# Gate and up products of a SwiGLU feed-forward: both parts of x side by side in one 512-column product

## The chip, the cores and the metric

One core of one Trainium2 chip runs the whole program in one launch. The metric is the device time of one execution in microseconds (us). TensorE (PE) multiplies, VectorE (DVE) and ScalarE (ACT) do the elementwise work, GpSimd (POOL) does a little, and SyncE (SP) issues the transfers.

## The reference

Two layers on 256 positions of width 1024. Each layer has a mixer (a gMLP spatial gate in layer 0, an RWKV-7 time mixer in layer 1) between two half-step feed-forwards, and a gated embedding at its end. So there are four feed-forwards, each with weights of its own:

```python
D_MODEL = 1024
D_FF = 2816
def rms_norm(x, g):
    y = xf * lax.rsqrt(jnp.mean(xf * xf, axis=-1, keepdims=True) + RMS_EPS)
    return (y * g.astype(jnp.float32)).astype(x.dtype)

def swiglu(x, w13, w2):
    gate, up = jnp.split(x @ w13, 2, axis=-1)
    return (jax.nn.silu(gate) * up) @ w2
...
    h = h + 0.5 * rms_norm(swiglu(rms_norm(h, g[0]), ffn_w13[i, 0], ffn_w2[i, 0]), g[1])
```

Everything is float32.

## The kernel before

**Products in parts.** A float32 operand is held as two parts, a high part rounded to the format in which TensorE takes a float32 in one pass, and a low part, the rest. A product is the sum of three: high by high, low by high and high by low. The helper `mm3` (lines 162 to 166) issues these three, on lines 164, 165 and 166, into one PSUM region.

**Weights.** They come in units of 128 rows by 1024 columns (512 KB). `emit_dma` reads a unit into a raw buffer. `emit_split` makes the two parts: ACT rounds it into the first half of a 2048-column slot (line 140), DVE subtracts to get the low part into the second half (line 142). `pump(k, reserve)` emits up to k splits if enough slots are free and at most 12 units are ahead; `need(i)` makes sure that unit i has been split, and `release(i)` gives its slot back.

**A feed-forward (`ffn`).** The hidden width of 2816 is walked in 11 chunks of 256; each chunk has a gate half and an up half. A chunk takes four units of gate and up weights (`at13`) and two units of down weights (`at2`). x, already scaled by the norm's gain and transposed, lies in two slots: one with the high parts, one with the low parts, each 8 blocks of 128 rows (k) by 256 positions. Chunks 0 and 1 go through `A`, where x is the stationary operand, and `TR` transposes their result. Chunks 2 to 10 go through `AT`, where the weights are stationary and the 256 positions are the moving operand, so that the result comes out transposed. `AT` takes two PSUM banks; bank j holds gate and up (256 columns each) of 128 hidden rows. For each of 8 blocks k, two j and two i (gate, up) it issues the three products of `mm3`: 96 products of 256 columns in a chunk, 36 chunks in the four feed-forwards. Then for each j it empties the bank: DVE multiplies the 512 columns by the positions' norm factors (line 387), ACT takes the silu (line 390), DVE multiplies gate by up (line 391), and the result is split into parts by ACT (line 393) and DVE (line 394) into a ring of four chunks.

`Dn(c, b)` multiplies a chunk of the ring by the down weights, 12 products of 512 columns for one half b of the positions, into two of four `acc` banks that stay open over all chunks. In the loop `Dn(c - 2, ...)` stands behind `AT(c)`. Behind the loop come `Dn` of chunks 8, 9 and 10 for the first half, the norm of that half, and the rest.

**Order.** The program is written in the order of the calls; a scheduler may move an instruction past neighbours on its engine, and each engine then runs its list in order, with waits where data or a buffer requires them. PSUM banks and slots are given out first freed, first taken.

Of the kernel before, what the change touches and what calls it, by code (L numbers as in the profile page):

```python
# [10 lines left out]
F32R = mybir.dt.float32r  # L11
AF = mybir.ActivationFunctionType
ALU = mybir.AluOpType
# [3 lines left out]
T = 256  # L17
NB = 2
KT = 8
DFF = 2816  # L20
FC = 11
# [20 lines left out]
SE, SO = CE[3] ** 0.5, CO[2] ** 0.5  # L42
BE, BO = CE[2] / (2 * SE), CO[1] / (2 * SO)
KE, KO = CE[1] - BE * BE, CO[0] - BO * BO


class Trunk:
    NSLOT = 20

    def __init__(self, ctx, tc, io):  # L50
        self.tc = tc
        self.nc = tc.nc
        self.io = io
        self.uid = 0
        ep = lambda name, bufs=1, **k: ctx.enter_context(tc.tile_pool(name=name, bufs=bufs, **k))
        self.slots = ep("slots")
        self.pp = ep("pp", space=bass.MemoryType.PSUM)
        self.rawp = ep("raw", 4)
        self.gp = ep("gp", 2)
        self.cp = ep("cp")  # L60
        self.sp = ep("sp", 2)
        self.rcp = ep("rc")
        self.rdp = ep("rd", space=bass.MemoryType.DRAM)
        self.free = deque(f"S{i}" for i in range(self.NSLOT))
        self.banks = deque(f"P{i}" for i in range(8))
        self.held = {}
        self.units = []
        self.hl = {}
        self.raw = {}
        self.n_dma = 0  # L70
        self.n_split = 0
        self.last = False
        self.left = [0, 1]
        self.on_pool = set()
        self.rn = [None, None]
        self.pq = {}
# [203 lines left out]
    def xslots(self):  # L280
        t = [self.slot("xT", F32R) for _ in range(2)]
        v = [q.rearrange("p (k t) -> p k t", t=T) for q in t]
        return t, [[q[:, :, b * 128:(b + 1) * 128] for q in v] for b in range(NB)]


    def ffn_units(self, f):
        io = self.io
# [18 lines left out]
    def ffn(self, l, j, at, filler=None):  # L306
        nc = self.nc
        at13, at2 = at
        gcol = l * 8 + 4 * j
        xs, xT, rstd = [], [], [None, None]  # L310
        hT = {}
        acc = {}

        def start(b):
            if b == 0:
                q, v = self.xslots()
                xs.extend(q)
                xT.extend(v)
            self.transpose_split(self.h[b], xT[b], gcol)
            rstd[b] = self.rn[b]  # L320

        yield start
        nxt = yield
        rs = [self.slot("hT", F32R) for _ in range(2)]
        ring = [q.rearrange("p (r s k t) -> p r s k t", r=2, s=2, t=T) for q in rs]
        hv = lambda c: ring[c % 4 // 2][:, c % 2]
        xv = [q.rearrange("p (k t) -> p k t", t=T) for q in xs]
        hc_of = {}

        def A(c, b, mid=None):  # L330

            ps = self.bank("mm")
            for u in range(4):
                if u == 3 and mid:
                    mid(1)
                wh, wl = self.need(at13[c] + u)
                for q in range(2):
                    k = 2 * u + q
                    sl = slice(q * 512, (q + 1) * 512)
                    self.mm3(ps, xT[b][0][:, k, :], xT[b][1][:, k, :], wh[:, sl], wl[:, sl], k == 0, k == KT - 1)  # L340
                if b == 1:
                    self.release(at13[c] + u)
            if rstd[b] is None:
                self.pre_norm(b)
                rstd[b] = self.rn[b]
            sg = self.small(256, "k1", 6)
            hc = self.small(256, "k1", 6)
            nc.scalar.activation(sg, ps[:, :256], AF.Silu, scale=rstd[b])
            nc.vector.scalar_tensor_tensor(hc, ps[:, 256:], rstd[b], sg, op0=ALU.mult, op1=ALU.mult)
            self.unbank(ps)  # L350
            hc_of[c, b] = hc

        def TR(c, b):
            v = hv(c)[:, :, :, b * 128:(b + 1) * 128]
            self.transpose_split(hc_of.pop((c, b)), (v[:, 0], v[:, 1]), None, 2)

        def rows():

            ps = self.bank("rb")
            for b in range(NB):  # L360
                d = self.small(256, "k1", 6)
                nc.vector.tensor_scalar(d[:, :128], self.ident, rstd[b], None, op0=ALU.mult)
                nc.tensor.matmul(ps[:, b * 128:(b + 1) * 128], lhsT=self.ones, rhs=d[:, :128], start=True, stop=True)
            r = self.small(256, "yc", 4)
            nc.scalar.copy(r, ps[:, :T])
            self.unbank(ps)
            return r

        def AT(c):

            ps = [self.bank("mm") for _ in range(2)]
            for u in range(4):
                wh, wl = self.need(at13[c] + u)
                for q in range(2):
                    k = 2 * u + q
                    for j in range(2):
                        for i in range(2):
                            sl = slice(q * 512 + i * 256 + j * 128, q * 512 + i * 256 + j * 128 + 128)
                            self.mm3(ps[j][:, i * T:(i + 1) * T], wh[:, sl], wl[:, sl], xv[0][:, k, :], xv[1][:, k, :],
                                     k == 0 and i == 0, k == KT - 1 and i == 1)  # L380
                self.release(at13[c] + u)
                if u % 2:
                    self.pump(1, self.room)
            for j in range(2):
                z = self.small(512, "pn", 3)
                sg = self.small(256, "k1", 6)
                nc.vector.tensor_tensor(z.rearrange("p (i t) -> p i t", i=2), ps[j].rearrange("p (i t) -> p i t", i=2),  # L387
                                        rbc.unsqueeze(1).to_broadcast([128, 2, T]), op=ALU.mult)
                self.unbank(ps[j])
                nc.scalar.activation(sg, z[:, :T], AF.Silu)  # L390
                nc.vector.tensor_tensor(sg, sg, z[:, T:], op=ALU.mult)
                hi, lo = hv(c)[:, 0, j, :], hv(c)[:, 1, j, :]
                nc.scalar.copy(hi, sg)
                nc.vector.tensor_tensor(lo, sg, hi.bitcast(F32), op=ALU.subtract)

        def Dn(c, b):
            if b not in acc:
                acc[b] = [self.bank("acc") for _ in range(2)]
            v = hv(c)[:, :, :, b * 128:(b + 1) * 128]
            order = [(k, n) for k in range(2) for n in range(2)]  # L400
            if c == FC - 1:
                order.sort(key=lambda q: q[1])
            for k, n in order:
                wh, wl = self.need(at2[c] + k)
                sl = slice(n * 512, (n + 1) * 512)
                self.mm3(acc[b][n], v[:, 0, k, :], v[:, 1, k, :], wh[:, sl], wl[:, sl],
                         c == 0 and k == 0, c == FC - 1 and k == 1)
            if b == 1:
                for k in range(2):
                    self.release(at2[c] + k)  # L410

        P = lambda k: self.pump(k, self.room)
        A(0, 0); P(2); A(1, 0, start); P(1)
        g = self.gain_tile(self.io["norm_g"][l, 1 + 4 * j:2 + 4 * j, :])
        TR(0, 0)
        A(0, 1); P(2); TR(1, 0)
        rbc = rows()
        A(1, 1); P(2); TR(0, 1)
        for c in range(2, FC):
            AT(c); P(1)  # L420
            if c == 2:
                TR(1, 1)
            if c < FC - 1:
                Dn(c - 2, 0); P(2)
                if c < FC - 2:
                    Dn(c - 2, 1); P(1)
        self.drop(*xs)
        Dn(FC - 3, 0)
        Dn(FC - 2, 0)
        Dn(FC - 1, 0)  # L430
        self.post_norm(0, acc[0], g, True, acc[0])
        P(2)
        Dn(FC - 4, 1)
        P(2)
        Dn(FC - 3, 1)
        P(2)
        Dn(FC - 2, 1)
        P(2)
        nxt(0)
        Dn(FC - 1, 1)  # L440
        self.drop(*rs)
        if filler is not None:
            filler()
        self.post_norm(1, acc[1], g, True, acc[1])
        yield
# [1069 lines left out]
def layout(inp):  # L1515

    c = np.ascontiguousarray
    f = lambda k: np.asarray(inp[k])
    a = {}
# [3 lines left out]
    a["norm_g"] = g  # L1523
    a["gT"] = g.reshape(16, KT, 128).transpose(2, 0, 1).reshape(128, 128)
    w = f("ffn_w13").reshape(4, 4, 2, 128, 2, FC, 256)
    a["w13"] = w.transpose(0, 5, 1, 3, 2, 4, 6).reshape(4, FC, 4, 128, 1024)
    a["w2"] = f("ffn_w2").reshape(4, 2 * FC, 128, D)
    a["wp"] = f("ple_w_proj")
    a["wg"] = f("ple_w_gate")
# [12 lines left out]
    s, t = np.arange(N)[:, None], np.arange(N)[None, :]  # L1542
# [32 lines left out]
```

## Time and profile before

| | |
|---|---|
| time, 3 runs | 1225.7, 1227.05, 1227.19 us; median 1227.05 |
| profiled execution | 1224.77 us |
| its span, first to last instruction | 1223.0 us |
| PE busy | 1191.8 us (97%), 8526 products |
| weight loads busy | 1027.2 us (84%) |
| DVE busy | 786.3 us (64%) |
| ACT busy | 603.6 us (49%) |
| products of 256 columns in `AT` | 3 x 1152 |

Busy time of PE is the time in which at least one product is under way. Successive products overlap, so the time that one product costs is read from the distance of the starts, or from a stretch divided by its count, and not from the duration of a row.

### The profile page before, as it was taken

Reading aid. Unit: us, or ns where it says so; the run is one execution under the profiler, and the core shown is the slowest. Engines: PE = TensorE matmul, PEld = TensorE weight load, DVE = VectorE, ACT = ScalarE, POOL = GpSimd, SP = SyncE. Lnnn points to the kernel's source line nnn. Section 1 sums busy time; section 2 is a strip of 40 time slices with the busy share of each in tenths; the row PEclk is TensorE's granted clock in tenths of the full one; section 3 lists DMA queues with packets and bytes.
Section 4 is the critical chain, followed back from the end, with each engine's and each line's share of the span. In section 5 each row is a group of like instructions: output and inputs, shape, how many; then the busy total and the mean of one; then the engine's idle time right before and its main releaser. Section 6 shows DMA issues by size and latency. Waiting matters only on the chain. (4 is left out here: it accounts for less than half of the span.)

```text
span 1223.0 us, 20881 instructions
## 1 busy us (share of the span) xinstructions
PE 1191.8 (97%) x8526; PEld 1027.2 (84%) x8526; DVE 786.3 (64%) x1129; ACT 603.6 (49%) x978; POOL 97.1 (8%) x109
## 2 busy tenths in 40 slices
PE   8999999999999999999999999989799899999997
PEld 7899998888889999987999996576575778999986
DVE  5775557686786556568665534699353988556563
ACT  6654446454574444368544422472162276444453
POOL 0000001000010000012000001300035420000011
PEclk9999999999999999999999999999799899999999
DMA  7985655555766555555755572103020368555510
GB/s 268 293 267 197 184 166 181 210 186 181 235 206 226 186 179 187 179 183 164 243 180 198 185 274 109 36 17 138 3 92 31 110 213 269 190 190 184 165 58 35
DMA packets 58786, 207.86 MB, mean 170 GB/s; under 512 B 6721, under 2 KB 7233, under 8 KB 58433
## 3 DMA queue, kind: packets, MB, share of 16 engines
q1 hardware_dynamic: 58688, 206.51, 51.1%
q8 instruction: 67, 1.10, 0.4%
q14 instruction: 31, 0.25, 0.1%
HBM read 205.44 MB, written 1.05 MB: 169 GB/s over the span
## 5 line engine op out<-in xcount | busy, mean ns | idle before, releaser
L142 DVE TENSOR_TENSOR w<-raw,w 128x1024 fp32r<-128x1024 f32 x335 | 408.2, 1224 | 255.0 <-ACT w L140 248.7
L140 ACT CAST w<-raw 128x1024 fp32r<-128x1024 f32 x340 | 356.5, 1052 | 335.1 <-PE mm L166 219.2
L164 PE MATMUL mm<-xT,w 128*128 128x256 f32 x1152 | 326.1, 283 | 0.0
L166 PE MATMUL mm<-xT,w 128*128 128x256 f32 x1152 | 326.0, 283 | 0.0
L165 PE MATMUL mm<-xT,w 128*128 128x256 f32 x1152 | 326.0, 283 | 0.0
L165 PEld LDWEIGHTS mm<-xT,w 128*128 128x128 f32 x1152 | 221.0, 192 | 1.3
L164 PEld LDWEIGHTS mm<-xT,w 128*128 128x128 f32 x1152 | 221.0, 192 | 1.3
L166 PEld LDWEIGHTS mm<-xT,w 128*128 128x128 f32 x1152 | 221.0, 192 | 0.0
L164 PE MATMUL acc<-w,hT 128*128 128x512 f32 x352 | 138.2, 393 | 0.0
L165 PE MATMUL acc<-w,hT 128*128 128x512 f32 x352 | 137.3, 390 | 0.0
L166 PE MATMUL acc<-w,hT 128*128 128x512 f32 x352 | 137.1, 389 | 0.0
L166 PEld LDWEIGHTS acc<-w,hT 128*128 128x128 f32 x352 | 66.1, 188 | 14.1
L164 PEld LDWEIGHTS acc<-w,hT 128*128 128x128 f32 x352 | 66.2, 188 | 12.6
L165 PEld LDWEIGHTS acc<-w,hT 128*128 128x128 f32 x352 | 66.3, 188 | 12.4
L218 POOL TENSOR_SCALAR rpost<-ss 128x1 f32<-128x1 f32 x15 | 7.4, 492 | 782.9 <-ACT junk L225 782.9
L387 DVE TENSOR_TENSOR pn<-mm,yc 128x512 f32<-128x512 f32 x72 | 47.4, 688 | 16.6 <-PE mm L166 16.6
L164 PE MATMUL mm<-w,xT 128*128 128x512 f32 x128 | 51.2, 410 | 3.4 <-ACT w L140 2.8
L165 PE MATMUL mm<-w,xT 128*128 128x512 f32 x128 | 51.2, 403 | 0.7 <-DVE xT L275 0.5
L166 PE MATMUL mm<-w,xT 128*128 128x512 f32 x128 | 50.4, 399 | 0.3 <-DVE w L142 0.3
L165 PE MATMUL z<-w,xT 128*128 128x512 f32 x128 | 49.9, 390 | 0.0
L166 PE MATMUL z<-w,xT 128*128 128x512 f32 x128 | 49.9, 390 | 0.0
L164 PE MATMUL z<-w,xT 128*128 128x512 f32 x128 | 49.7, 393 | 0.0
(275 smaller groups left out, 1639.5 us busy)
## 6 DMA issues: line engine op xcount, KB each, us to landing
raw<-in_w SPq DMA_DIRECT2D x264, 512.0 KB, 4.3
raw<-in_win SPq DMA_DIRECT2D x32, 512.0 KB, 3.9
wf<-in_wrkv SPq DMA_DIRECT2D x12, 1024.0 KB, 7.3
raw<-in_wout SPq DMA_DIRECT2D x16, 512.0 KB, 4.3
raw<-in_wg SPq DMA_DIRECT2D x16, 512.0 KB, 3.4
gbc<-in_norm_g SPq DMA_DIRECT2D x9, 512.0 KB, 4.9
raw<-in_bwout SPq DMA_DIRECT2D x8, 512.0 KB, 3.5
bin<-in_bin SPq DMA_DIRECT2D x8, 256.0 KB, 4.2
```

The source lines that it names most:

```text
L140: self.high = self.nc.scalar.copy(hh, r[:p, :n])
L142: eng.tensor_tensor(ll, r[:p, :n], hh.bitcast(F32), op=ALU.subtract)
L164: mm(out, lhsT=lh, rhs=rh, start=start, stop=False)
L165: mm(out, lhsT=ll, rhs=rh, start=False, stop=False)
L166: mm(out, lhsT=lh, rhs=rl, start=False, stop=stop)
L218: nc.gpsimd.tensor_scalar(r, a, b, eps, op0=ALU.add, op1=ALU.add)
L387: nc.vector.tensor_tensor(z.rearrange("p (i t) -> p i t", i=2), ps[j].rearrange("p (i t) -> p i t", i=2), rbc.unsqueeze(1).to_broadcast([1 ...
```

## The change

The slots of x change their layout: slot 0 holds blocks 0 to 3, slot 1 blocks 4 to 7, and in each block the 256 high parts and the 256 low parts lie beside each other (`xpairs`; the class `Halves` lets `A` and the transposes index the two slots as before). In `AT` the high part of a weight tile is now multiplied by all 512 columns of a block (high by high into the first half of a bank, high by low into the second), and the low part by the 256 high columns, into the first half. So j is the outer loop, gate and up have a bank each, and the host lays the weight units of chunks 2 to 10 out so that two units serve j = 0 and two serve j = 1. When the banks of one j are full, ACT copies the second half of each into z, DVE adds the first half, and DVE then multiplies z by the norm factors; the rest is as before.

```diff
+class Halves:
+    def __init__(self, *parts):
+        self.parts = parts
+
+    def __getitem__(self, ix):
+        p, k, t = ix
+        if isinstance(k, slice):
+            i = k.start // 4
+            return self.parts[i][p, k.start - 4 * i:k.stop - 4 * i, t]
+        return self.parts[k // 4][p, k % 4, t]
...
+    def xpairs(self):
+
+        t = [self.slot("xT", F32R) for _ in range(2)]
+        v = [q.rearrange("p (k s t) -> p k s t", k=4, s=2) for q in t]
+        return t, [[Halves(*(q[:, :, s, b * 128:(b + 1) * 128] for q in v)) for s in range(2)] for b in range(NB)]
...
             if b == 0:
-                q, v = self.xslots()
+                q, v = self.xpairs()
                 xs.extend(q)
...
-        xv = [q.rearrange("p (k t) -> p k t", t=T) for q in xs]
...
         def AT(c):
 
-            ps = [self.bank("mm") for _ in range(2)]
-            for u in range(4):
-                wh, wl = self.need(at13[c] + u)
-                for q in range(2):
-                    k = 2 * u + q
-                    for j in range(2):
+
+            for j in range(2):
+                ps = [self.bank("mm") for _ in range(2)]
+                for u in range(2):
+                    wh, wl = self.need(at13[c] + 2 * j + u)
+                    for q in range(4):
+                        k = 4 * u + q
+                        x = xs[u][:, q * 512:(q + 1) * 512]
                         for i in range(2):
-                            sl = slice(q * 512 + i * 256 + j * 128, q * 512 + i * 256 + j * 128 + 128)
-                            self.mm3(ps[j][:, i * T:(i + 1) * T], wh[:, sl], wl[:, sl], xv[0][:, k, :], xv[1][:, k, :],
-                                     k == 0 and i == 0, k == KT - 1 and i == 1)
-                self.release(at13[c] + u)
-                if u % 2:
-                    self.pump(1, self.room)
-            for j in range(2):
+                            sl = slice(q * 256 + i * 128, q * 256 + i * 128 + 128)
+                            nc.tensor.matmul(ps[i], lhsT=wh[:, sl], rhs=x, start=k == 0, stop=False)
+                            nc.tensor.matmul(ps[i][:, :T], lhsT=wl[:, sl], rhs=x[:, :T], start=False, stop=k == KT - 1)
+                    self.release(at13[c] + 2 * j + u)
+                self.pump(1, self.room)
                 z = self.small(512, "pn", 3)
                 sg = self.small(256, "k1", 6)
-                nc.vector.tensor_tensor(z.rearrange("p (i t) -> p i t", i=2), ps[j].rearrange("p (i t) -> p i t", i=2),
-                                        rbc.unsqueeze(1).to_broadcast([128, 2, T]), op=ALU.mult)
-                self.unbank(ps[j])
+                for i in range(2):
+                    zi = z[:, i * T:(i + 1) * T]
+                    nc.scalar.copy(zi, ps[i][:, T:])
+                    nc.vector.tensor_tensor(zi, ps[i][:, :T], zi, op=ALU.add)
+                self.unbank(*ps)
+                z2 = z.rearrange("p (i t) -> p i t", i=2)
+                nc.vector.tensor_tensor(z2, z2, rbc.unsqueeze(1).to_broadcast([128, 2, T]), op=ALU.mult)
                 nc.scalar.activation(sg, z[:, :T], AF.Silu)
...
-    a["w13"] = w.transpose(0, 5, 1, 3, 2, 4, 6).reshape(4, FC, 4, 128, 1024)
+    w13 = w.transpose(0, 5, 1, 3, 2, 4, 6).reshape(4, FC, 4, 128, 1024)
+    w = f("ffn_w13").reshape(4, 2, 4, 128, 2, FC, 2, 128)
+    wT = w.transpose(0, 5, 6, 1, 3, 2, 4, 7).reshape(4, FC, 4, 128, 1024)
+    a["w13"] = np.concatenate([w13[:, :2], wT[:, 2:]], 1)
```

## Rows read from the trace of the kernel before

**Rows 1.** The page, parts 1 and 2: busy time of the engines; granted clock in 40 slices.
```profile
PE 1191.8 (97%) x8526; PEld 1027.2 (84%) x8526; DVE 786.3 (64%) x1129; ACT 603.6 (49%) x978; POOL 97.1 (8%) x109
PEclk9999999999999999999999999999799899999999
```

**Rows 2.** The page, costliest groups: busy us, mean ns of one, idle before them.
```profile
L164 PE MATMUL mm<-xT,w 128*128 128x256 f32 x1152 | 326.1, 283 | 0.0
```

**Rows 3.** Busy time by stretch: length, each engine's busy us, clock, DMA share, GB/s.
```profile
37.21:48.80 11.59, 11.59 (x99) 11.59 (x98) 8.38 (x9) 7.00 (x9) 0.00 (x0) 1.00 0.88 278
54.51:66.02 11.51, 11.51 (x98) 11.51 (x96) 8.62 (x10) 6.47 (x7) 0.00 (x0) 1.00 0.92 303
1154.79:1166.30 11.51, 11.51 (x97) 11.51 (x96) 5.24 (x8) 3.88 (x5) 0.00 (x0) 1.00 0.42 138
66.02:71.49 5.47, 5.47 (x27) 4.51 (x25) 4.18 (x6) 3.54 (x5) 0.00 (x0) 1.00 0.89 330
1166.30:1182.66 16.36, 16.36 (x75) 13.48 (x74) 9.40 (x15) 8.71 (x17) 1.72 (x4) 1.00 0.15 49
386.07:403.05 16.98, 16.98 (x122) 16.02 (x121) 10.01 (x13) 7.66 (x10) 0.00 (x0) 1.00 0.59 187
54.51:71.49 16.98, 16.98 (x122) 16.02 (x120) 12.80 (x15) 10.01 (x12) 0.00 (x0) 1.00 0.91 311
```

**Rows 4.** Timeline of PE where the two shapes meet: start, duration in us.
```profile
65.90 0.28 PE L166 MATMUL mm<-xT,w 128*128 128x256 f32 x1
66.02 0.40 PE L164 MATMUL acc<-w,hT 128*128 128x512 f32 x1
66.25 0.40 PE L165 MATMUL acc<-w,hT 128*128 128x512 f32 x1
...
71.26 0.39 PE L166 MATMUL acc<-w,hT 128*128 128x512 f32 x1
71.49 0.28 PE L164 MATMUL mm<-xT,w 128*128 128x256 f32 x1
71.60 0.28 PE L165 MATMUL mm<-xT,w 128*128 128x256 f32 x1
```

**Rows 5.** Timeline of the weight loads in the same `AT`, and the last before `Dn`.
```profile
65.78 0.19 PEld L166 LDWEIGHTS mm<-xT,w 128*128 128x128 f32 x1
65.90 0.19 PEld L164 LDWEIGHTS acc<-w,hT 128*128 128x128 f32 x1
```

**Rows 6.** Instructions of a line or tile: duration in ns, least, median, most.
```profile
L348 ACT ACTIVATE k<-mm,rpre x16: 462/474/489, 18.5 to 1023.5; 128x256 f32<-128x256 f32 x16
L349 DVE SCALAR_TENSOR_TENSOR k<-mm,rpre,k x16: 476/479/486, 19.8 to 1024.7; 128x256 f32<-128x256 f32 x16
L387 DVE TENSOR_TENSOR pn<-mm,yc x72: 682/685/693, 49.5 to 1166.5; 128x512 f32<-128x512 f32 x72
L391 DVE TENSOR_TENSOR k<-k,pn x72: 416/420/425, 52.1 to 1168.9; 128x256 f32<-128x256 f32 x72
L393 ACT CAST hT<-k x72: 388/407/409, 52.6 to 1169.4; 128x256 fp32r<-128x256 f32 x72
```

**Rows 7.** Timeline of ACT: a copy of 256 columns out of PSUM.
```profile
34.52 0.37 ACT L365 COPY yc<-rb 128x256 f32<-128x256 f32 x1 [1.40 <-PE rb L363]
```

**Rows 8.** Timelines of ACT, DVE and PE behind the last `AT` of feed-forward 0.
```profile
182.24 1.05 ACT L140 CAST w<-raw 128x1024 fp32r<-128x1024 f32 x1 [1.67 <-PE mm L165]
...
183.32 1.23 DVE L142 TENSOR_TENSOR w<-raw,w 128x1024 fp32r<-128x1024 f32 x1 [0.27 <-ACT w L140]
...
185.13 1.22 DVE L142 TENSOR_TENSOR w<-raw,w 128x1024 fp32r<-128x1024 f32 x1
186.27 0.75 DVE L394 TENSOR_TENSOR hT<-k,hT 128x256 fp32r<-128x256 f32 x2
...
188.53 0.39 PE L165 MATMUL acc<-w,hT 128*128 128x512 f32 x1
```

**Rows 9.** Timeline of DVE: the second bank of the first `AT` is emptied.
```profile
52.46 0.68 DVE L387 TENSOR_TENSOR pn<-mm,yc 128x512 f32<-128x512 f32 x1
```

## The prediction

> **What bounds the kernel now.** I read the page's first two parts, then the costliest groups, then busy time by stretch, and only then single instructions. The first part shows PE under way for 1191.8 of 1223.0 us and DVE and ACT for 64% and 49%; the second shows the clock at its upper level (2.4 GHz) nearly throughout [rows 1]. A busy PE is no proof of a full PE, so the groups matter more: the 3 x 1152 products of 256 columns in `AT` have no idle time in front of them [rows 2]. The stretches give the price. One `AT` is 96 products in 11.51 us, 119.9 ns each; 32 of the 36 are 11.51 or 11.52 us long (the last stands in the rows), three of those that come first in a feed-forward 11.59, and the fourth of these has three of its products moved ahead. One pair of `Dn` is 24 products of 512 columns in 5.47 us, 227.9 ns each, and 72 in a row take 16.36 us, 227.2 ns each [rows 3]. In both PE is busy for the whole stretch: what ends last there is PE's own stream, and no weight, buffer or other engine. So about 36 x 11.5 = 415 us, a third of the time, is priced by the products of `AT` alone.
>
> **What a product costs.** 256 more columns cost 227.5 - 119.9 = 107.6 ns (I take 227.5, the middle of the two stretches); so columns account for 107.6 of the 119.9 ns, and 12.3 ns are paid once for each product with its weight load, however wide it is.
>
> **The change on PE.** For one weight tile `AT` issues three products of 256 columns now and one of 512 and one of 256 then: 768 columns either way, one product and one load fewer. A tile goes from 3 x 119.9 = 359.7 to 227.5 + 119.9 = 347.4 ns. There are 32 tiles in a chunk: 11.51 becomes 11.12 us, 0.39 less. Times 36 chunks (1152 tiles x 12.3 ns): **-14.1 us**. With 227.9 it would be -13.7, with 227.2 -14.5.
>
> The trace of before holds no long alternation of the two shapes, so the pair has to be bounded. From below: if the fixed part vanished wherever the shapes alternate, a tile would cost 768 x 107.6 / 256 = 322.8 ns, 36.9 less than now, -42.5 us. From above: a load takes 0.19 us by its row [rows 5], longer than a 256-column product; if it could not start before that product and had to be over before the next began, a tile would cost 227.5 + 190 = 417.5 ns, +66.6 us. The nearest rows are the places where the shapes meet [rows 4]: 256 to 512 at 65.90 and 66.02, 0.12 us apart; 512 to 512, 0.23; 512 to 256 at 71.26 and 71.49, 0.23; 256 to 256, 0.11. Each product costs its own width whatever follows it. The load rows say why the upper end is unlikely: loads start every 0.12 us though each lasts 0.19, and the load for the first 512-column product starts at 65.90, with the last 256-column product, and that does not hold the 512-column one at 66.02 up [rows 4, 5]. I take the sum of the two prices.
>
> By the Trainium skill ("TensorE: Matmul & The Clock Gate", section "Back-to-back issue gap") a product alone costs its columns at 2.4 GHz and about 2.5 ns. By that figure, as an estimate, 1152 products fewer are worth 2.9 us. The stretches show 12.3 ns, and by the measured price it is 14.1.
>
> **What emptying a bank adds.** For each j: two copies of 256 columns out of PSUM on ACT, two adds of 256 columns on DVE, and the norm multiply reads SBUF in place of PSUM. A copy of this shape takes 0.37 us [rows 7], a silu out of PSUM 0.47 [rows 6]. An add with one operand in PSUM lies between 0.42 (both in SBUF, line 391) and 0.48 (line 349); the multiply between 0.685 (line 387, the same shape) and 2 x 0.42 = 0.84. I take the lower value for the copy, its own operation, and 0.45 and 0.69 for the other two. Per chunk that is 4 x 0.37 = 1.5 us more on ACT and 4 x 0.45 = 1.8 more on DVE, at the upper ends 1.9 and 2.2; over 36 chunks 53 (68) us of ACT and 65 (80) us of DVE.
>
> All of it lies beside PE. A settled stage (`AT` and its two `Dn`) is 16.98 us of PE with 10.01 of DVE and 7.66 of ACT; it becomes 16.6 with some 11.8 and 9.2. The fullest stage is in feed-forward 0, where weights are still catching up: 12.80 becomes 14.6 of 16.6 on DVE and 10.01 becomes 11.5 on ACT [rows 3]. No engine reaches PE's time. The units are used in the same order, two released before each `pump`, so splits and their DMAs keep their places, one unit for 2.78 instead of 2.88 us of PE. The added wait is the copy of j = 0, in the middle of a chunk: ACT's next split is queued behind it, and DVE's behind the add. That holds splits up until j = 0 is done, in a stage with over 7 us free on ACT; PE does not see it. If that cover were gone, the 3.3 us of a chunk would show, but only once DVE's 11.8 (14.6) us had passed 16.6.
>
> **Where the cover is thin.** Two places. (a) Behind the last `AT` of a feed-forward no `Dn` of an older chunk is left but 24 products, and then chunk 10 itself is wanted. In feed-forward 0 that `AT` ends at 182.16 (where the 72 products of `Dn` begin), DVE writes the last low part until 187.02, with one cast on ACT and two splits on DVE taken in between, and PE reads it at 188.53 [rows 8]: 1.5 us spare. Then, j = 0 is done early, and j = 1 alone needs, in a row, two copies 0.74, add 0.45, multiply 0.69, silu and cast 0.41 each (ACT over 256 columns of SBUF), multiply and subtract 0.42 each [rows 6]: 3.5 us. With the same cast and two splits in between, 1.05 + 1.23 + 1.22, it is 7.0, and with some 0.1 us for each of six changes of engine 7.6, against 6.37 that PE leaves: 1.2 us late, if all of these fall in the chain; two of them fit. I take no stall and keep 4 x 1.2 = 4.8 us. (b) In feed-forward 0 the second bank of the first `AT` is emptied from 52.46 to 53.14, 4.3 us after that `AT` ended at 48.80 [rows 3, 9], late because ACT's casts wait for transfers. By the order of banks, the second `AT` then takes a bank of the first's j = 1 5.7 us after its end. Copies and adds in place of one multiply may be 1 us later: 0 to 1 us, once.
>
> **Sum.** The profiled execution took 1224.77 us (span 1223.0 and 1.8 around it): 1224.77 - 14.1 = 1210.7. The median of the runs shown is 2.28 us above the profiled one, so on the scale of the median 1227.05 - 14.1 = **1213.0 us**.
>
> **Rivals.** *Part is given back.* Places (a) and (b) both stall: 4.8 + 1.0 = 5.8 us, 1218.8. For it: the 1.5 us spare and the longer chain. Against it: half the old chain, j = 0, leaves that stretch. *No gain.* If a product's price went by columns alone (119.9 ns per 256, 239.8 per 512), 768 columns would cost the same and the time would stay at 1227. Against it: 512 columns cost 227.2 to 227.9 wherever they stand. The Trainium skill's 2.5 ns of the page named above leans this way and would give 1224.1. *Slower.* Loads exposed: if the load for the next 512-column product could not run beside the 256-column one before it, each tile would pay up to 190 ns on top of 227.5; the loss begins once the 256-column product takes over 132.2 ns in place of 119.9, and at full size it is 1227.05 + 66.6 = 1294. For it: the load's row is longer than the product that should hide it, and the alternation is new. Against it: [rows 4, 5] and the stream of 256-column products, which hides such loads at every step. *A change that does nothing* can be left out: the products are counted in the program.
>
> **Chances.** Forecast 80%, with a range of its own from 1210.5 to 1216 (the two prices of 512 columns, runs that differ by 1.5 us, a stall or two); part given back 11%; no gain 3%; slower 6%. The range that should hold 8 in 10 reaches into the first rival: 1210 to 1219. A measurement of this kernel can tell 0.2%, 2.5 us, from no change. Faster by more: the first two cases, 0.91; within: 0.03; slower: 0.06.
>
> **What would show it.** In the trace after, an `AT` of 64 products in 11.1 us with PE busy throughout; starts 0.23 and 0.12 us apart in turn; some 7374 products in all (8526 - 1152). ACT up by 53 to 68 us and DVE by 65 to 80, with no idle of PE named after them in the 36 chunks. Place (a) is wrong if the first products of chunk 10's `Dn` wait for `hT`. The prediction is wrong as a whole if starts in `AT` are 0.23 and clearly over 0.12 apart, or if PE waits for weights inside a chunk.

## The result

The changed kernel took 1217.1 us (median; 1216.46 to 1223.09) against 1226.4 of the kernel before, ratio 0.9939 with a 95% interval of 0.991 to 0.9967. A second time it was 1217.6 against 1226.1, ratio 0.9931 (0.9909 to 0.9953). Forecast were 1213.0, with 1210.5 to 1216 as the range of the forecast itself and 1210 to 1219 as the wide one. The direction was right and the wide range held, but the narrow one did not: of 14.1 us the medians show 9.3 and 8.5, and the streams of products, added up below, 7.0.

The page of the changed kernel, engines and the groups that answer to [rows 1, 2] (busy us and mean ns of one before the second bar, idle before them behind it):

```profile
PE 1188.6 (97%) x7374; PEld 966.8 (79%) x7374; DVE 839.2 (69%) x1273; ACT 652.3 (53%) x1122; POOL 97.7 (8%) x109
...
L400 PE MATMUL mm<-xT,w 128*128 128x512 f32 x1152 | 408.5, 399 | 0.0
L401 PE MATMUL mm<-xT,w 128*128 128x256 f32 x1152 | 323.4, 281 | 0.0
...
L408 ACT COPY pn<-mm 128x256 f32<-128x256 f32 x144 | 48.6, 373 | 87.9 <-PE mm L401 87.9
L409 DVE TENSOR_TENSOR pn<-mm,pn 128x256 f32<-128x256 f32 x144 | 54.7, 420 | 36.1 <-ACT pn L408 36.1
...
L412 DVE TENSOR_TENSOR pn<-pn,yc 128x512 f32<-128x512 f32 x72 | 49.8, 691 | 2.1
```

There are 1152 products fewer, as forecast. Those of `AT` still have no idle time before them, though ACT works 49 us and DVE 53 us more. So the shortfall is no wait. Busy time by stretch (`AT` of the fourth chunk of feed-forward 1, its two `Dn`, and both together):

```profile
386.47:397.76 11.29, 11.29 (x65) 9.79 (x64) 8.07 (x10) 5.65 (x9) 0.00 (x0) 1.00 0.61 190
397.76:403.26 5.50, 5.50 (x26) 4.51 (x25) 3.44 (x8) 3.41 (x6) 0.00 (x0) 1.00 0.58 174
386.47:403.26 16.79, 16.79 (x89) 14.30 (x88) 11.52 (x17) 9.06 (x14) 0.00 (x0) 1.00 0.60 185
```

`AT` is 11.29 us, 0.22 less than in [rows 3], not 0.39; a pair of products costs 11.29 / 32 = 352.8 ns, not 347.4. A pair of `Dn`, whose code is the same, is 5.50 in place of 5.47 us. The timeline of PE shows where the 5.4 ns are:

```profile
64.05 0.40 PE L400 MATMUL mm<-xT,w 128*128 128x512 f32 x1
64.29 0.28 PE L401 MATMUL mm<-xT,w 128*128 128x256 f32 x1
64.40 0.40 PE L400 MATMUL mm<-xT,w 128*128 128x512 f32 x1
64.63 0.28 PE L401 MATMUL mm<-xT,w 128*128 128x256 f32 x1
64.75 0.40 PE L400 MATMUL mm<-xT,w 128*128 128x512 f32 x1
64.99 0.28 PE L401 MATMUL mm<-xT,w 128*128 128x256 f32 x1
65.11 0.40 PE L400 MATMUL mm<-xT,w 128*128 128x512 f32 x1
```

Three pairs take 1.06 us. From a wide product to the next low one it is 0.24, 0.23 and 0.24 us, over all 1152 places 236 ns in the mean; from a low one to the next wide one 117 ns. In long runs of their own width they cost 226.7 ns (`Dn` from its sixth product on in the trace of before, and wide products only, below) and 120.0 (`AT` before): the wide product pays 9 ns more, the low one gets 3 back.

The whole can be added up in the streams. From the first `AT` to the start of the last three `Dn` of the first half a feed-forward took 144.95 us before and takes 143.20 now (144.59 and 142.84 in the last, whose first chunk begins earlier); the sum over four, called the streams' sum below, is 579.4 and 572.5, **7.0 us less**: 36 x 0.22 = 8.0 less in `AT` and 1.0 more in the `Dn` of the loop. The medians differ by 9.3 and 8.5 us, and 7.0 lies within both intervals. What lies between the feed-forwards varies from execution to execution by more than this leaves open: the stretch with the RWKV mixer took 287.0 to 292.3 us in profiled executions of kernels that don't differ there (294.1 with wide products only, below), and the time up to the first `AT` 36.6 to 40.7 (39.6 and 40.7 with the changed kernel, 36.6 to 38.0 with its other orders, which begin alike).

### The profile page after: what moved, and what is told of

Read it like the earlier page. It is cut to its first block, busy times and chain, and to the rows that moved or that the text cites. A ratio compares the mean times of both kernels' runs of the same rounds, so it can differ in the third digit from the quotient of the medians.

```text
span 1221.2 us, 18852 instructions
## 1 busy us (share of the span) xinstructions
PE 1188.6 (97%) x7374; PEld 966.8 (79%) x7374; DVE 839.2 (69%) x1273; ACT 652.3 (53%) x1122; POOL 97.7 (8%) x109
## 5 line engine op out<-in xcount | busy, mean ns | idle before, releaser
L400 PE MATMUL mm<-xT,w 128*128 128x512 f32 x1152 | 408.5, 399 | 0.0
L401 PE MATMUL mm<-xT,w 128*128 128x256 f32 x1152 | 323.4, 281 | 0.0
L400 PEld LDWEIGHTS mm<-xT,w 128*128 128x128 f32 x1152 | 216.4, 188 | 53.4
L401 PEld LDWEIGHTS mm<-xT,w 128*128 128x128 f32 x1152 | 217.6, 189 | 1.3
L408 ACT COPY pn<-mm 128x256 f32<-128x256 f32 x144 | 48.6, 373 | 87.9 <-PE mm L401 87.9
L409 DVE TENSOR_TENSOR pn<-mm,pn 128x256 f32<-128x256 f32 x144 | 54.7, 420 | 36.1 <-ACT pn L408 36.1
L289 DVE SCALAR_TENSOR_TENSOR xT<-tr,gT,xT 128x128 fp32r<-128x128 f32 x112 | 35.7, 346 | 23.9 <-ACT xT L288 23.1
L412 DVE TENSOR_TENSOR pn<-pn,yc 128x512 f32<-128x512 f32 x72 | 49.8, 691 | 2.1
L179 PE MATMUL z<-w,xT 128*128 128x512 f32 x128 | 49.9, 390 | 0.0
L180 PE MATMUL z<-w,xT 128*128 128x512 f32 x128 | 49.9, 390 | 0.0
```

The source lines that it names most:

```text
L179: mm(out, lhsT=ll, rhs=rh, start=False, stop=False)
L180: mm(out, lhsT=lh, rhs=rl, start=False, stop=stop)
L289: nc.vector.scalar_tensor_tensor(lo, v, gc, hi.bitcast(F32), op0=ALU.mult, op1=ALU.subtract))
L400: nc.tensor.matmul(ps[i], lhsT=wh[:, sl], rhs=x, start=k == 0, stop=False)
L401: nc.tensor.matmul(ps[i][:, :T], lhsT=wl[:, sl], rhs=x[:, :T], start=False, stop=k == KT - 1)
L408: nc.scalar.copy(zi, ps[i][:, T:])
```

## The experiments

All edits are made to the changed kernel; the times stand against the kernel before, run on the same chip.

**The changed kernel again, and three orders of its products.** Expected of the kernel as it is:

> The changed kernel as it is, beside the variants. In its first trace a chunk of AT took 11.29 us (352.8 ns for a pair of products), 0.22 less than before, and the four feed-forwards together came out 6.9 us shorter; forecast were 14.1. Theory A (a switch of width costs: a 512-column product that follows a 256-column one pays some 9 ns more than in a run of its own kind), theory B (the wide product in AT costs about 236 ns whatever stands beside it, because of its operands or the traffic around it) and theory C (a product pays when it adds into the bank that the product just before it wrote) all expect the same here: AT 11.29 us, time 1216 to 1218 us, 6 to 10 us under the kernel before.

Measured: 1217.6 us, ratio 0.9931; `AT` 11.29 us and the streams' sum 572.5 us, each equal to the first trace's.

Runs of two: high by high and low for gate and up, then the two low products.

```diff
                         for i in range(2):
                             sl = ...
                             nc.tensor.matmul(ps[i], lhsT=wh[:, sl], rhs=x, ...)
+                        for i in range(2):
+                            sl = ...
                             nc.tensor.matmul(ps[i][:, :T], lhsT=wl[:, sl], rhs=x[:, :T], ...)
```

> Per block k the two products with the high weights (512 columns) come first, then the two with the low weights (256): half as many switches of width, the same products and loads. Theory A: half of the 6.4 ns of excess per pair goes, AT 11.19 us, 3.5 us less over 36 chunks than the changed kernel. Theory B: AT stays 11.29 us. Theory C: successive products alternate between the two banks, the excess goes wholly, AT 11.09 us.

Runs of sixteen: for each j all the wide products, then all the low ones; both units are given back at the end.

```diff
-                for u in range(2):
-                    wh, wl = self.need(at13[c] + 2 * j + u)
-                    for q in range(4):
-                        k = 4 * u + q
+                ws = [self.need(at13[c] + 2 * j + u) for u in range(2)]
+                for part in range(2):
+                    for k in range(KT):
...
```

> For each j all 16 products with the high weights, then all 16 with the low weights: two switches to the wide product in a chunk in place of 32. A unit's slot comes free later, at the end of j. Theory A: nearly all of the excess goes, AT 11.10 to 11.16 us, 5 to 7 us less over 36 chunks than the changed kernel, 1210 to 1212 us if the later slots cost nothing. Theory B: AT 11.29 us, no gain. Theory C: as A, 11.09 us.

Crossed banks: one wide product of the second bank goes first, then wide products of one bank alternate with low products of the other (`wide` and `low` are helpers that issue one product each).

```diff
...
+                    if u == 0:
+                        wide(1, 0, w)
                     for q in range(4):
...
+                        wide(0, 4 * u + q, w)
+                        low(1, 4 * u + q, w)
+                    for q in range(4):
+                        if u or q:
+                            wide(1, 4 * u + q, w, ...)
+                        low(0, 4 * u + q, w, ...)
```

> The widths alternate as in the changed kernel, but a low product adds into the other bank than the wide product before it, so that no product adds into the bank that was written just before (but for two places in each half). Theory A: AT 11.25 to 11.30 us, as the changed kernel. Theory B: the same. Theory C: AT 11.09 to 11.12 us.

Busy time of `AT` and its `Dn` in the same chunk, for runs of two, for runs of sixteen and for crossed banks:

```profile
382.21:393.34 11.13, 11.13 (x65) 9.71 (x64) 8.02 (x10) 5.47 (x8) 0.00 (x0) 1.00 0.61 193
393.34:398.80 5.46, 5.46 (x27) 4.52 (x25) 3.48 (x8) 3.48 (x6) 0.00 (x0) 1.00 0.63 181
```

```profile
382.10:393.21 11.11, 11.11 (x66) 9.83 (x64) 6.67 (x9) 4.97 (x8) 0.00 (x0) 1.00 0.65 203
393.21:398.68 5.47, 5.47 (x27) 4.51 (x26) 4.04 (x7) 3.25 (x7) 0.00 (x0) 1.00 0.59 179
```

```profile
384.04:395.32 11.28, 11.28 (x65) 9.80 (x64) 8.06 (x10) 5.47 (x8) 0.00 (x0) 1.00 0.63 190
395.32:400.77 5.45, 5.45 (x26) 4.51 (x25) 3.43 (x8) 3.48 (x6) 0.00 (x0) 1.00 0.59 177
```

The reader is to compare the first number of each line behind the window: the same 64 products take 11.13, 11.11 or 11.28 us by their order alone. Theory B (the wide product costs 236 ns in any case) and theory C (the bank written just before) fall: with crossed banks the pair stays at 235.6 + 117.1 ns. Theory A holds in its direction, and the order of widths is the cause; its size for runs of two does not hold (11.19 us expected, three quarters of the excess gone instead of half). Times: runs of two 1209.3 us, ratio 0.9866 (0.9839 to 0.9893); runs of sixteen 1210.9, 0.9871 (0.9837 to 0.9904); crossed 1215.8, 0.9922 (0.9893 to 0.995). The streams' sum for runs of two is 565.4 us, 14.1 less than before. That this is the number forecast for the change is chance: `AT` gives 13.4 of it, since a pair still costs 348.0 ns and not 347.4, and the `Dn` of the loop 0.6, which was not forecast.

**The emptying alone.** Three products of 256 columns again, with the new layouts and the new emptying:

```diff
-                            nc.tensor.matmul(ps[i], lhsT=wh[:, sl], rhs=x, start=k == 0, stop=False)
-                            nc.tensor.matmul(ps[i][:, :T], lhsT=wl[:, sl], rhs=x[:, :T], start=False, stop=k == KT - 1)
+                            nc.tensor.matmul(ps[i][:, :T], lhsT=wh[:, sl], rhs=x[:, :T], start=k == 0, stop=False)
+                            nc.tensor.matmul(ps[i][:, :T], lhsT=wl[:, sl], rhs=x[:, :T], start=False, stop=False)
+                            nc.tensor.matmul(ps[i][:, T:], lhsT=wh[:, sl], rhs=x[:, T:], start=False, stop=k == KT - 1)
```

> Only the emptying is changed: the new layouts of x and of the weights and the new emptying (copy, add, multiply) stay, but each tile has three products of 256 columns again, with the high-by-low one in the second half of the bank. My theory (the emptying lies wholly beside PE, the shortfall of the change is in the order of the widths): AT 11.51 us as before, 120 ns per product, the four feed-forwards within 0.5 us of the kernel before, time 1225 to 1228 us, ratio 0.998 to 1.002. Rival (the added ACT and DVE work slows PE's reads or its start, and that is where the shortfall came from): products over 120 ns, AT 11.6 to 11.7 us, 4 to 7 us slower than before.

Busy time by stretch, the same chunk, `AT` and then the whole stage:

```profile
386.33:397.84 11.51, 11.51 (x97) 11.51 (x96) 8.11 (x10) 5.66 (x9) 0.00 (x0) 1.00 0.59 185
...
386.33:403.31 16.98, 16.98 (x121) 16.02 (x120) 11.53 (x17) 9.07 (x14) 0.00 (x0) 1.00 0.57 187
```

PE's time is that of [rows 3] to the last digit, with DVE and ACT 1.5 and 1.4 us busier in the stage; ratio 1.0008 (0.9993 to 1.0024). The streams' sum is 579.4 us as before. So the emptying costs PE nothing, and the traffic beside it is not the cause.

**Wide products only.** The line with `wl` is left out.

> The products with the low weights are left out of AT (that part of the computation is missing): 32 products of 512 columns in a chunk and no 256-column one. My theory: without a switch of width a wide product in AT costs 226.7 to 227.5 ns, AT 7.26 to 7.28 us. Rival (the wide product in AT costs more because of its operands): 236 ns, AT 7.55 us. If PE is still what ends last, the time falls by 36 x 4.2 = 152 us against the kernel before; if ACT or DVE takes over, by less.

```profile
354.80:362.05 7.25, 7.25 (x33) 6.01 (x32) 6.74 (x9) 5.27 (x8) 0.00 (x0) 1.00 0.86 286
```

`AT` 7.25 us, 226.7 ns a product: a wide product with these operands is no dearer than one of `Dn`. The time, in a single run, was 1087 us; PE now waits in places, for the emptying among others, so it says nothing on the price.

**Runs of four, and a snake.** In the first, wide and low change places in every second block; in the second, in every second unit (`for part in ((0, 1) if u == 0 else (1, 0))`).

```diff
+                        for part in ((0, 1) if q % 2 == 0 else (1, 0)):
+                            for i in range(2):
...
```

> The order of wide and low turns round from block to block, so that widths come in runs of four (two at the ends of j). Runs of one gave AT 11.29 us, of two 11.14, of sixteen 11.12. If each return to the wide product costs what it did for runs of two (2.9 ns in all), AT is 11.11 to 11.13 us; if it costs what it did for runs of sixteen (some 20 ns), AT is 11.20 to 11.25 us and the time 1212 to 1215.

> Per j: 8 wide, 16 low, 8 wide, with each unit still given back in the middle. The next stretch (the other j, or Dn with its 512 columns) then begins behind wide products. Two returns to the wide width per chunk, as with runs of sixteen: AT 11.11 to 11.14 us, and Dn 5.45 in place of 5.48, since it no longer begins behind a low product. Time as the other two orders with runs, 1208 to 1211 us; a rival by which only the first product after a switch matters would expect the same AT but Dn unchanged at 5.48.

`AT` and `Dn` for runs of four, then for the snake:

```profile
383.29:394.50 11.21, 11.21 (x65) 9.80 (x64) 8.04 (x10) 5.47 (x8) 0.00 (x0) 1.00 0.63 194
394.50:399.97 5.47, 5.47 (x25) 4.50 (x24) 3.45 (x8) 3.48 (x6) 0.00 (x0) 1.00 0.55 164
```

```profile
382.14:393.28 11.14, 11.14 (x66) 9.84 (x64) 8.05 (x10) 5.47 (x8) 0.00 (x0) 1.00 0.60 189
393.28:398.72 5.44, 5.44 (x26) 4.50 (x24) 3.45 (x8) 3.48 (x6) 0.00 (x0) 1.00 0.55 174
```

Runs of four are worse than runs of two: 11.21 us and a streams' sum of 568.8 (565.4); ratio 0.9907 (0.9878 to 0.9935). Of the two values expected the higher one came. So the cost does not go by the number of switches. Set against 11.09 (32 pairs of 346.7 ns), the excess for each return to the wide width is 6 ns behind one low product (0.20 / 32), 3 behind two (0.04 / 16), 15 behind four (0.12 / 8) and some 20 behind sixteen (snake, 0.04 / 2). The snake's `AT` and time came out as expected: 11.14 us, ratio 0.9866 (0.9837 to 0.9896). Its `Dn` takes 5.44 us, but that decides little, since `Dn` takes 5.45 or 5.46 with crossed banks and runs of two, where it does begin behind a low product. The streams' sums of runs of sixteen and of the snake are 564.9 and 565.1 us: within 0.5 us of runs of two, and the times don't tell the three apart.

**Other widths of the low product.** The order stays as in the changed kernel; `:T` in the low product becomes `:384` (a term more) or `:192` (a term less).

> The order of the changed kernel, wide and low in turn, but the low weights multiply 384 columns (the 256 high ones and 128 of the low ones, a term that is left out otherwise). By columns and 13 ns for each product a pair is 226.7 + 173.3 = 400.0 ns. Theory L (the excess comes from a product too short for the load that runs beside it: the transposes of 128 columns in the trace of before follow each other at 109 ns, where their columns alone would be 53, so a load needs about 109 ns and a 256-column product leaves little room): no excess, 400 ns, AT 12.80 us. Theory S (any switch of width costs): 405 to 407 ns, AT 12.96 to 13.02 us.

> The order of the changed kernel, but the low weights multiply only 192 of the 256 high columns (the low part of the weights is left out for 64 positions). By columns and 13 ns each a pair is 226.7 + 93.3 = 320.0 ns. Theory L: the low product is now shorter than the 109 ns of a load, so the excess grows: 338 to 345 ns a pair, AT 10.8 to 11.0 us. Theory S: 325 to 327 ns, AT 10.40 to 10.47 us.

`AT` by stretch and the timeline of PE, 384 columns, then 192; for 192 the weight loads too:

```profile
402.77:415.77 13.00, 13.00 (x65) 11.60 (x64) 8.25 (x10) 5.72 (x9) 0.00 (x0) 1.00 0.56 168
...
404.80 0.39 PE L400 MATMUL mm<-xT,w 128*128 128x512 f32 x1
405.03 0.34 PE L401 MATMUL mm<-xT,w 128*128 128x384 f32 x1
405.20 0.40 PE L400 MATMUL mm<-xT,w 128*128 128x512 f32 x1
...
406.01 0.40 PE L400 MATMUL mm<-xT,w 128*128 128x512 f32 x1
```

```profile
385.90:396.75 10.85, 10.85 (x65) 9.54 (x64) 7.74 (x10) 5.63 (x9) 0.00 (x0) 1.00 0.59 193
...
387.91 0.42 PE L400 MATMUL mm<-xT,w 128*128 128x512 f32 x1
388.17 0.25 PE L401 MATMUL mm<-xT,w 128*128 128x192 f32 x1
388.25 0.42 PE L400 MATMUL mm<-xT,w 128*128 128x512 f32 x1
...
389.27 0.42 PE L400 MATMUL mm<-xT,w 128*128 128x512 f32 x1
...
388.17 0.19 PEld L400 LDWEIGHTS mm<-xT,w 128*128 128x128 f32 x1
388.28 0.19 PEld L401 LDWEIGHTS mm<-xT,w 128*128 128x128 f32 x1
```

With 384 columns a pair takes 406 ns (13.00 us for 32), 6 over the sum of the two prices: theory L, by which a longer low product would hide its neighbour's load, falls there, and theory S holds. With 192 a pair takes 340 ns (1.36 us for four), 20 over, which theory L expected and theory S did not: 14 more than with 256, close to the 16 ns by which 93 ns falls short of the 109 ns at which loads follow each other in the transposes. The load rows bear this out: with 192 columns the load of the low product starts 0.11 us behind the load before it, and 26 ns after the wide product beside it has started; with 256 and 384 columns it starts 3 ns after it. So the runs are read as two costs that add: some 6 ns for the alternation, and a floor by the load once the product is shorter than it; only one such width was run. The formula of the Trainium skill ("TensorE: Matmul & The Clock Gate", section "LDWEIGHTS (loading the stationary operand)"), columns over 1.2, makes an estimated 107 ns of 128 columns. The distance of 109 ns agrees with it; the row of a load lasts 0.19 us.

**The better order once more.**

> The order in runs of two once more, in five rounds, as the version that should beat both kernels: AT 11.14 us, ratio to the kernel before 0.984 to 0.989, where the changed kernel had 0.9931 and 0.9939.

1211.5 us, ratio 0.9883 (0.9866 to 0.9899); `AT` 11.14 us, streams 565.4. The two intervals of the changed kernel are 0.991 to 0.9967 and 0.9909 to 0.9953: runs of two beat both kernels.

## Why the prediction was right, and where its size was off

- *PE bounds `AT`*: right. The 0.22 us that PE saved in a chunk shows in the stretch, and 2.9 us a stage more of DVE and ACT (11.52 and 9.06 against 10.01 and 7.66) do not.
- *12.3 ns for each product with its load*: right, and if anything low. Long runs show 226.7 and 120.0 ns, 13.3 more than 512 and 256 columns at 2.4 GHz. By the 2.5 ns of the Trainium skill ("TensorE: Matmul & The Clock Gate", section "Back-to-back issue gap") the gain would have been an estimated 2.9 us; the streams show 7.0, and 14.1 in the better order.
- *"I take the sum of the two prices"*: the step that was mis-sized. A pair in turn costs 352.8 ns, not 347.4: 5.4 x 1152 = 6.2 us given back, and 1.0 more in `Dn` (5.50 us behind the alternating `AT`, 5.47 behind that of before). 14.1 - 6.2 - 1.0 = 6.9. The bounds held it, but the value was taken from single places where the widths meet, read to 0.01 us, and "each product costs its own width whatever follows it" does not hold: what a product costs depends on those before it. The hint was in the trace of before: `Dn` behind `AT` takes 227.9 ns a product, 72 in a row 227.2. Taken together the two stretches give 226.9 ns and some 25 ns paid once, which is what a return to the wide width costs, and I put a middle value in its place. The starts in that trace show it: behind a settled `AT` the first five products of `Dn` take 233, 236, 228, 233 and 231 ns, then 227. This would still not have given the size, for 32 returns at 25 ns would be 0.8 us a chunk, where 0.2 was given back. The sign set for being wrong, a low product clearly over 0.12 us, watched the other product of the pair: the surcharge is on the wide one.
- *Emptying hidden*: right. The copies cost 0.37 us as taken, the adds 0.42 (taken: 0.45). ACT and DVE grew by 49 and 53 us, less than the 53 to 68 and 65 to 80 forecast, because the sum took each row in full, while two successive copies take 0.67 us together and two adds 0.75.
- *Place (a), behind the last `AT`*: no stall, as taken, though splits did fall into the chain. DVE wrote the last low part until 188.14, PE read it at 189.17, 1.0 us spare in place of 1.5:

```profile
187.71 0.43 DVE L417 TENSOR_TENSOR hT<-k,hT 128x256 fp32r<-128x256 f32 x1 [0.47 <-ACT hT L416]
...
189.17 0.39 PE L179 MATMUL acc<-w,hT 128*128 128x512 f32 x1
```

- *Place (b), the bank of the first `AT`*: no stall in the changed kernel (adds done at 54.64, the next `AT` starts at 56.64). The place is real: with the shorter `AT` of 192 columns PE waited there 3.8 us, and the products behind the wait ran at half the clock (starts 0.49 and 0.16 us apart; granted clock 0.50, that is 1.2 GHz):

```profile
58.89 0.79 PE L400 MATMUL mm<-xT,w 128*128 128x512 f32 x1 [3.77 <-DVE pn L409]
...
60.28 0.68 PE L400 MATMUL mm<-xT,w 128*128 128x512 f32 x1
60.77 0.36 PE L401 MATMUL mm<-xT,w 128*128 128x192 f32 x1
60.92 0.68 PE L400 MATMUL mm<-xT,w 128*128 128x512 f32 x1
```

- *The rivals*: part was given back, but not at the places named for it. That the wide range held is therefore luck in part: it reached to 1219 for stalls at (a) and (b), which did not come. Exposed loads in the full size of that rival, 66.6 us, did not come either.

What stays open: why a change of width costs at all, and why two low products in a row are cheaper than one or four. By these runs neither the bank, nor the operands, nor the traffic, nor the load's time alone explains it; what TensorE does between a load and the products around it is not in these traces.

## What to carry to other kernels

Where PE's own stream is the bound, count products as well as columns: merging two products that share a weight tile saved 6 ns a tile as it was first written and 12 in a better order (7.0 and 14.1 us over 1152 tiles), at no cost beside PE. Then look at the order: the same 64 products took 11.29 or 11.13 us, so group products of a width, and try more than one length of run. Runs of two, of sixteen and the snake were alike here, runs of four were worse. Take the price of a mixed stream from a stretch that is mixed, not from the two pure ones.

## What the runs showed of the hardware

An alternation of widths cost some 6 ns a pair with 256 and with 384 columns, and the price of a return to the wide product was not monotone in the number of low ones before it (6, 3, 15, about 20 ns for one, two, four, sixteen). The price is not paid by one product: behind sixteen low products the first five wide ones took 233, 236, 228, 232 and 231 ns before they settled at 227, and behind sixteen wide ones the first two low ones took 113 and 119 ns before they settled at 120. That is 27 ns lost and 8 won, 19 in all, close to the 20 of the long runs. In shorter runs the next change comes before the last one has settled: in strict turn the wide products take 241, 236 and 232 ns and the low ones 120, 113 and 118, over and over.
